# Two-layer hybrid encoder: norm factor of the differential heads by DMA, another order of output tiles, sink as a score column

## The chip, the cores and the metric

The kernel runs on one NeuronCore of a Trainium2 chip. It has a matrix engine (TensorE, PE in the profile, with PEld for its weight loads), a vector engine (DVE), an activation engine (ACT), a general-purpose engine (POOL) and a queue engine (SP) that issues all the DMAs here. Each engine works through its own list of instructions in order and waits on semaphores. The metric is the device time in microseconds of the whole program, median over runs. Three runs of the kernel before took 1253.59 to 1255.1 us, with a median of 1253.75.

## The reference

A two-layer encoder on x of 1024 tokens by 1024 channels in float32, with 256 memory tokens. Each layer: RMS norm, one input projection, several groups of attention heads, a SiLU gate on their outputs, an output projection, and the residual; at the end one more RMS norm.

Layer 0 has three groups of heads of width 64. (A) six windowed heads over 128 tokens to either side, with a relative-position bias and a learned sink logit per head that takes part in the softmax only as an extra column:

```
sink_col = broadcast(sink)                       # one column
p = softmax(concat([logits, sink_col], -1))[..., :-1]
```

(B) six dense heads with RMS-normed queries and keys and rotary positions. (X) four cross-attention heads into the memory.

Layer 1 has (C) six differential heads with values of width 128, and (X) again:

```
p = softmax(s + bias)            # two score maps, i = 0, 1
w = p[0] - lam * p[1]
y_c = rmsnorm(w @ v, subln_g) * (1 - lam_init)
```

so each row of a differential head's output is divided by its own root mean square over 128 channels. That factor is one number per token and head.

## The kernel before, in words

Everything large is computed with split operands: each float32 operand is a high part and a low part, and three matmuls (high-high, high-low, low-high) stand for one (`load_w`, `split_to`). The input projections run as jobs (class `Jobs`) in 24 matmuls per 128 output channels and 512 tokens, into one of two PSUM banks of the ring `A` (`ps_a`, L222). Scores go into one of two double banks of the ring `S` (`ps_s`), and transposes and small results into one of two banks of the ring `T` (`ps_t`).

`run_steps` (L441) goes through the attention as a list of steps; a step is a query block of 128 tokens (B, C, X) or two (A). In iteration i it issues, in this order: the copy `er<-e` of step i-1's probabilities by DMA (`hop`), the scores of step i (`s1`), a share of the projection jobs, the pending follow-ups of earlier steps (`posts`, one piece of each per iteration), the product with the values of a step some iterations back (`s3`), the transposes of step i-2 (`s2`, tile `te`, split by ACT into `PTh` and by DVE into `PTl`), the end of step i's softmax (`finish`), and more jobs. From this program order a scheduler makes each engine's list; it can move an instruction past others.

**Layer 0, B step** (L1044-1070): DVE takes the minimum `mn` of the scores, multiplies it by the query's norm factor into `mr` (L1063), and ACT takes the exponential with `mr` as bias (L1064). **A step** (L1116-1151): DVE adds bias and takes the minimum together with the sink (L1132), ACT takes the exponential and its sum `z` (L1136), then the exponential of the sink, `es` (L1139); DVE adds `es` to `z` (L1141) and takes the reciprocal.

**Layer 1, C step** (L1412-1452) with `s3` at every second step (L1457): 24 matmuls give `oc`, 128 channels by 256 tokens. Follow-up `d1`, one iteration later, sums the squares over the channels with four matmuls (`ssqc`, L1479), two ACT instructions add the epsilon term (L1483) and POOL raises to -1/2 (`rz`, L229). This leaves the factors as a column per block, one token per partition. Follow-up `d2`, another iteration later, has TensorE transpose each column, broadcast to 128x128, so that every partition holds the row of all 128 factors (`rbcc`, L1492); DVE multiplies `O` by it out of PSUM (L1494), and POOL multiplies by the gate (L1497). After the last block of a head the gated output is stored to DRAM (`store_y`).

**Output projection** (`out_proj`, L1216): eight tiles of 128 tokens, in the order `ORD[l]`. Stored outputs come back by DMA (`yr`) and are split; each tile has 48 matmuls of 512 columns. For the tiles in `PRE[l]` a part was already done as filling work during the attention (`pre`, L687): in layer 0 tiles 2 to 5 have 24 matmuls left and tiles 6 and 7 have 12; in layer 1 tiles 2, 3 and 4 have 12 left. `pieces` (L1230) chooses the PSUM banks: a double bank of `S` for all but the last tile, and single banks of `A` and `T` for the last. After a tile's matmuls DVE adds the residual (`x`, L1274), ACT squares and sums (L1275), POOL raises to -1/2, and DVE scales (`xs`, L1295). In layer 0 the scaled tile is then transposed (`tx`, L344) into layer 1's input.

## Time and profile before

| | |
|---|---|
| median of 3 runs | 1253.75 us (1253.59 to 1255.1) |
| profiled execution, its own time | 1255.58 us |
| its span, first to last instruction | 1253.8 us |
| granted TensorE clock | 0.996 |
| busy: PE / DVE / ACT / POOL | 96% / 65% / 51% / 33% |
| layer 0 attention | about 100 to 540 us |
| layer 0 output projection | about 540 to 600 us |
| layer 1 projections, cross-attention | about 600 to 720 us |
| layer 1 differential attention | about 720 to 1184 us |
| layer 1 output projection | about 1184 to 1254 us |

A row of a timeline gives the start in us, the duration, the engine, the source line, the operation, `out<-in`, and in brackets the idle time before it with what ended it. A row of groups gives count, busy time, mean ns of one, and idle time before. In the rows on DMAs come the count, the size of each and the median us from issue to landing.

### The profile page before, as it was taken

How to read it: one execution, taken by the hardware profiler on the slowest of the kernel's cores; microseconds unless marked ns; L12 is line 12 of the kernel's file. 1: busy time of each engine (PE TensorE's matmuls, PEld its weight loads, DVE VectorE, ACT ScalarE, POOL GpSimd, SP SyncE). 2: the span in 40 equal slices, each digit the busy share in tenths (PEclk: the TensorE clock that was granted, in tenths of full speed). 3: DMA queues.
4: the chain of work that ended last, by engine and by line, in shares of the span. 5: the costliest groups of instructions: out<-in, count | busy, mean ns of one | idle time of the engine just before them, and what ended most of it. 6: DMA issues, size and time to landing. Idle time of an engine off the chain costs nothing. (4 is left out here: it accounts for less than half of the span.)

```text
span 1253.8 us, 19637 instructions
## 1 busy us (share of the span) xinstructions
PE 1205.5 (96%) x6806; PEld 999.2 (80%) x6806; DVE 817.1 (65%) x1545; ACT 640.2 (51%) x1395; POOL 413.5 (33%) x390
## 2 busy tenths in 40 slices
PE   5999999999998999998999999999999999999997
PEld 4887788888887787887888778788887878877876
DVE  5547666377778788746355865766667666678444
ACT  6249654256666766533157644444444454456322
POOL 5023456266666565403122212212122131223100
PEclk9999999999999999999999999999999999999999
DMA  6654444545365575466644334243342433445363
GB/s 252 198 187 149 155 168 150 171 155 201 148 224 191 210 246 186 154 203 213 185 163 144 125 107 120 93 143 108 105 137 76 136 115 118 144 151 189 129 211 118
DMA packets 96350, 199.90 MB, mean 159 GB/s; under 512 B 11478, under 2 KB 31190, under 8 KB 96252
## 3 DMA queue, kind: packets, MB, share of 16 engines
q1 hardware_dynamic: 96252, 198.65, 47.4%
q8 instruction: 54, 0.88, 0.3%
q14 instruction: 44, 0.36, 0.1%
HBM read 79.32 MB, written 31.47 MB: 88 GB/s over the span
## 5 line engine op out<-in xcount | busy, mean ns | idle before, releaser
L297 PE MATMUL acc<-h,wh 128*128 128x512 f32 x1536 | 499.1, 399 | 7.3 <-DVE yt L624 3.1
L297 PEld LDWEIGHTS acc<-h,wh 128*128 128x128 f32 x1536 | 283.2, 188 | 73.3 <-issue 13.4
L297 PE MATMUL acc<-h,wl 128*128 128x512 f32 x768 | 304.6, 397 | 1.8 <-POOL wl L241 1.8
L241 POOL TENSOR_TENSOR wl<-wr,wh 128x512 fp32r<-128x512 f32 x96 | 124.9, 1302 | 340.0 <-DVE wh L239 125.2
L316 DVE TENSOR_TENSOR PTl<-te,PTh 128x512 fp32r<-128x512 f32 x224 | 148.2, 687 | 131.2 <-ACT PTh L315 128.4
L1440 ACT ACTIVATE e<-e,mn 128x1024 f32<-128x1024 f32 x96 | 110.2, 1149 | 130.7 <-DVE mn L1437 127.5
L297 PEld LDWEIGHTS acc<-h,wl 128*128 128x128 f32 x768 | 144.8, 189 | 35.5 <-issue 4.4
L315 ACT CAST PTh<-te 128x512 fp32r<-128x512 f32 x224 | 124.9, 591 | 30.2 <-PE te L540 24.6
L1068 POOL TENSOR_TENSOR e<-e,rz 128x1024 f32<-128x1024 f32 x48 | 91.7, 1913 | 78.1 <-DVE rz L1067 66.7
L1437 DVE CUSTOM_DVE_ANT_0 e<-sc,toep 128x1024 f32<-128x1024 f32 x96 | 113.9, 1217 | 5.3 <-PE sc L1431 5.0
L540 PEld LDWEIGHTS te<-identr,er 128*128 128x128 f32 x896 | 91.8, 143 | 21.1 <-issue 4.1
L540 PE MATMUL te<-identr,er 128*128 128x128 f32 x896 | 100.0, 246 | 7.5 <-issue 3.2
L239 DVE CAST wh<-wr 128x512 fp32r<-128x512 f32 x112 | 59.1, 530 | 43.9 <-PE acc L297 14.4
L1064 ACT ACTIVATE e<-sb,mr,nrq 128x1024 f32<-128x1024 f32 x48 | 58.0, 1208 | 48.4 <-DVE mr L1063 33.9
L1449 DVE SCALAR_TENSOR_TENSOR e<-e,mr 128x1024 f32<-128x1024 f32 x48 | 76.2, 1588 | 1.3
L1464 PE MATMUL oc<-PTh,v 128*128 128x256 f32 x384 | 74.8, 288 | 0.3 <-DVE ckl L1333 0.3
L660 PE MATMUL po<-woh,yh 128*128 128x512 f32 (+1 forms) x172 | 65.9, 383 | 1.5 <-DVE x L1274 1.5
L660 PE MATMUL po<-woh,yl 128*128 128x512 f32 (+1 forms) x172 | 65.6, 381 | 0.0
L660 PE MATMUL po<-wol,yh 128*128 128x512 f32 (+1 forms) x172 | 65.5, 381 | 0.0
L1464 PEld LDWEIGHTS oc<-PTh,v 128*128 128x128 f32 x384 | 61.5, 192 | 0.7 <-DVE ckl L1333 0.6
L1059 DVE TENSOR_REDUCE mn<-sb 128x1 f32<-128x1024 f32 x48 | 58.4, 1216 | 5.1 <-PE sb L509 4.7
L318 ACT ACTIVATE yh<-yr 128x256 fp32r<-128x256 f32 (+2 forms) x56 | 24.0, 448 | 67.3 <-DMA yr<-ysc 38.5
(199 smaller groups left out, 2247.1 us busy)
## 6 DMA issues: line engine op xcount, KB each, us to landing
er<-e SPq DMA_DIRECT2D x112, 512.0 KB, 2.9
wr<-in_w_in SPq DMA_DIRECT2D x96, 256.0 KB, 2.8
ysc<-gy SPq DMA_DIRECT2D x16, 512.0 KB, 2.9
wor<-in_w_out SPq DMA_DIRECT2D x32, 256.0 KB, 3.5
cq<-sg SPq DMA_DIRECT2D x64, 128.0 KB, 2.6
ck<-sg SPq DMA_DIRECT2D x48, 128.0 KB, 2.3
er<-e SPq DMA_DIRECT2D x12, 384.0 KB, 2.8
xpsc<-xh SPq DMA_DIRECT2D x18, 256.0 KB, 2.5
```

The lines of the kernel that those rows point to most:

```text
L239: nc.vector.tensor_copy(hi, raw)
L241: (nc.vector if fast else nc.gpsimd).tensor_tensor(out=lo, in0=raw, in1=hi, op=ALU.subtract)
L297: lastmm[0] = nc.tensor.matmul(acc, a, b[:, k, c0:c0 + n], start=(i == 0), stop=(i == 23))
L315: nc.scalar.copy(hi, src)
L316: return nc.vector.tensor_tensor(out=lo, in0=src, in1=hi, op=ALU.subtract)
L540: nc.tensor.transpose(to[:, i * P:(i + 1) * P], e[0][:, k * P:(k + 1) * P], idt)
L660: lastmm[0] = nc.tensor.matmul(acc, a, b, start=(start and n == 0), stop=(stop and n == 2))
L1068: nc.gpsimd.tensor_tensor(out=et, in0=et, in1=rz.to_broadcast([P, 1024]), op=ALU.mult)
L1437: nc.vector.tensor_tensor_reduce(out=et, in0=Sp, in1=toeps[h][:, w0:w0 + 1024], scale=1.0, scalar=BIG, op0=ALU.add, op1=ALU.min, accum_out ...
L1440: nc.scalar.activation(et, et, AF.Exp, bias=mn[:, m:m + 1], scale=-1.0, accum_out=z[:, m:m + 1])
L1449: nc.vector.scalar_tensor_tensor(out=es[0], in0=es[1], scalar=c, in1=es[0], op0=ALU.mult, op1=ALU.add)
L1464: nc.tensor.matmul(acc, V[:, kt, v, :], pt[:, kt, :], start=(n == 0), stop=(n == 23))
```

## The change

Five edits. (1) The row of norm factors reaches all partitions through DRAM: `d1` ends by storing the two columns to `rc_d`, transposed, and `d2` loads them back into `sqc` (whose squares are no longer needed), broadcast to all partitions; the multiply becomes a third follow-up `d3`, one iteration later. The last pair of the last head keeps the transposes. (2) The third tile of an output projection uses the two single banks of `A`. (3) Both orders of output tiles are others. (4) In a B step ACT computes `mr`. (5) In an A step the sink is written by ACT as one more score column behind each block's scores, the exponential and its sum run over that column too, and the separate exponential and addition go; the tile has 770 columns instead of 768.

```
-ORD = ((0, 1, 2, 3, 4, 5, 6, 7), (0, 1, 4, 2, 5, 3, 6, 7))
+ORD = ((0, 1, 2, 6, 3, 7, 4, 5), (0, 1, 5, 2, 6, 3, 4, 7))
...
-                nc.vector.tensor_tensor(out=mr, in0=mn, in1=rq[:, qb, h:h + 1], op=ALU.mult)
+                nc.scalar.activation(mr, mn, AF.Identity, scale=rq[:, qb, h:h + 1])
...
-                et = new_e(M)[:, :768].rearrange("p (j c) -> p j c", j=2)
+                et = new_e(M)[:, :770].rearrange("p (j c) -> p j c", j=2)
...
+                ends = [(min(8, qb + 2) - qb + 1) * P for qb in (2 * p, 2 * p + 1)]
+                if ends[0] == ends[1]:
+                    nc.scalar.copy(et[:, :, ends[0]], nsink[:, h:h + 1].to_broadcast([P, 2]))
+                else:
+                    for j in range(2):
+                        nc.scalar.copy(et[:, j, ends[j]:ends[j] + 1], nsink[:, h:h + 1])
...
-                    nc.scalar.activation(et[:, j, c:c + n], et[:, j, c:c + n], AF.Exp,
+                    nc.scalar.activation(et[:, j, c:c + n + 1], et[:, j, c:c + n + 1], AF.Exp,
                                          bias=mn[:, j:j + 1], scale=-1.0, accum_out=z[:, j:j + 1])
-                es = stat("es", 2)
-                nc.scalar.activation(es, mn, AF.Exp, bias=sinkb[:, h:h + 1], scale=1.0)
                 def finish():
-                    nc.vector.tensor_tensor(out=z, in0=z, in1=es, op=ALU.add)
...
-                t = M.at.tile([P, 1024], F32R, tag="er", name="er", bufs=M.cfg["er"])[:, :768]
-                a, b = (P if p == 0 else 0), (768 - P if p == 3 else 768)
+                t = M.at.tile([P, 1024], F32R, tag="er", name="er", bufs=M.cfg["er"])[:, :770]
+                a, b = (P if p == 0 else 0), (769 - P if p == 3 else 769)
...
         def pieces(i):
+            if i == 2:
+                p = [(ps_a("po")[:, 0:512], c, 512) for c in (0, 512)]
+                return p, p
...
+                    short = h == 5 and qb == 7
...
                         rstd_from(r, v, 2)
                         st_["r"] = r
+                        if not short:
+                            st_["d"] = dr.tile([2, P], F32, name="rc_d")
+                            dma(st_["d"].rearrange("t p -> p t"), r)
 
                     def d2():
-                        T = ps_t("rbcc")
-                        for i in range(2):
-                            nc.tensor.transpose(T[:, i * P:(i + 1) * P],
-                                                st_["r"][:, i:i + 1].to_broadcast([P, P]), ident)
-                        nc.vector.scalar_tensor_tensor(out=O, in0=O, scalar=gs, in1=T[:, 0:256],
+                        dma(sq, st_["d"].rearrange("t p -> (t p)").partition_broadcast(P))
+
+                    def d3():
+                        if short:
+                            T = ps_t("rbcc")[:, :256]
+                            for i in range(2):
+                                nc.tensor.transpose(T[:, i * P:(i + 1) * P],
+                                                    st_["r"][:, i:i + 1].to_broadcast([P, P]), ident)
+                        else:
+                            T = sq
+                        nc.vector.scalar_tensor_tensor(out=O, in0=O, scalar=gs, in1=T,
                                                        op0=ALU.mult, op1=ALU.mult)
...
-                    return [d1, d2]
+                    return [d1, d3] if short else [d1, d2, d3]
```

How the lists of instructions change is shown at three places. First, TensorE in layer 1's attention, at a pair of query blocks of the second head; `acc` is the projection job that fills the time, `oc` the product with the values. Before:

```order
L297 MATMUL acc<-h,wh 128x512 x2
L297 MATMUL acc<-h,wl 128x512
L1492 MATMUL rbcc<-ident,rz_9444 128x128 x2
L1464 MATMUL oc<-PTh,v 128x256
L1464 MATMUL oc<-PTl,v 128x256
L1464 MATMUL oc<-PTh,v 128x256 x2
```

With the change:

```order
L297 MATMUL acc<-h,wh 128x512 x2
L297 MATMUL acc<-h,wl 128x512
L1470 MATMUL oc<-PTh,v 128x256
L1470 MATMUL oc<-PTl,v 128x256
L1470 MATMUL oc<-PTh,v 128x256 x2
```

The two transposes are gone and nothing else has moved here.

Second, SP's queue in the same stage, over some four query blocks (`er` the copy of the probabilities, `wr` a weight load, `ysc` the store of a finished head, `ck` rows of the next head's keys). Before:

```order
L175 DMA wr<-in_w_in 128x512 x2
L175 DMA er<-e 128x1024 x2
L175 DMA wr<-in_w_in 128x512 x2
L175 DMA er<-e 128x1024
L175 DMA ysc_95<-gy 128x1024
```

With the change:

```order
L175 DMA wr<-in_w_in 128x512 x2
L175 DMA rc_d<-rz_9629 128x2x1
L175 DMA sqc<-rc_d 128x256
L175 DMA er<-e 128x1024 x2
L175 DMA wr<-in_w_in 128x512
L175 DMA rc_d<-rz_9818 128x2x1
L175 DMA sqc<-rc_d 128x256
L175 DMA wr<-in_w_in 128x512
L175 DMA er<-e 128x1024
L175 DMA ysc_95<-gy 128x1024
```

Store and load of a pair stand back to back here, ahead of copies and a weight load; at other pairs a weight load, copies or key rows stand between the two.

Third, ACT in layer 0's attention, around A steps and the B steps between them (`yt` and `PT` are the work of earlier steps). Before:

```order
L1136 ACTIVATE e,z_3389<-e,mn_3388 128x384 x2
L1139 ACTIVATE es<-mn_3388,small 128x2
L437 COPY yt<-oa 64x256
L315 CAST PTh<-te 128x4x128 x2
L425 ACTIVATE gy<-acc 128x512
L315 CAST PTh<-te 128x4x128
L1064 ACTIVATE e,z<-sb,mr,nrq 128x1024
L315 CAST PTh<-te 128x4x128
```

With the change:

```order
L1142 ACTIVATE e,z_3380<-e,mn_3379 128x385 x2
L437 COPY yt<-oa 64x256
L315 CAST PTh<-te 128x4x128 x2
L425 ACTIVATE gy<-acc 128x512
L1063 ACTIVATE mr<-mn,rq 128x1
L315 CAST PTh<-te 128x4x128
L1064 ACTIVATE e,z<-sb,mr,nrq 128x1024
```

The exponential of the sink is gone, the exponentials are a column longer, and the scaling `mr` stands ahead of a cast and the B step's exponential. The copies of the sink (`e<-nsink`) stand ahead of the exponentials of their step, here some rows earlier.

## Prediction

> **What bounds the kernel now.** The page's engine shares come first, then the table by stretch, then who waited for whom.
>
> ```profile
> PE 1205.5 (96%) x6806; PEld 999.2 (80%) x6806; DVE 817.1 (65%) x1545; ACT 640.2 (51%) x1395; POOL 413.5 (33%) x390
> ```
>
> ```profile
> 200.00:540.00 340.00, 329.17 (x1974) 280.27 (x1974) 242.59 (x528) 200.96 (x442) 191.49 (x171) 0.99 0.55 190
> 545.00:600.00 55.00, 50.97 (x254) 41.42 (x253) 36.60 (x58) 21.11 (x43) 13.19 (x16) 1.00 0.66 206
> 800.00:1100.00 300.00, 300.00 (x1689) 242.82 (x1688) 206.32 (x361) 141.71 (x280) 65.68 (x66) 1.00 0.36 117
> 1100.00:1184.00 84.00, 81.37 (x477) 65.68 (x475) 62.72 (x111) 47.24 (x101) 20.31 (x19) 1.00 0.47 160
> ```
>
> In the table by stretch the columns are the stretch, its length, the busy time (and count) of PE, PEld, DVE, ACT and POOL, the clock, the DMA share and GB/s. PE is the bound everywhere, and in layer 1's attention, 800 to 1100 us, it never rests: 300.00 of 300. What leaves PE's list there shortens the program one for one, and what is only taken off DVE, ACT or POOL there gives nothing. Elsewhere PE has little idle time: 340.00 - 329.17 = 10.8 us in layer 0's attention and 55.00 - 50.97 = 4.0 us in layer 0's output projection. The waits of PE say whose it is:
>
> ```profile
> PE te L540 <- issue: 3.2, 5, 1.4
> PE sa L509 <- ACT e L1064: 2.1, 2, 1.1
> PE sa L509 <- DVE mn L1132: 1.7, 3, 1.1
> PE tx L344 <- DVE h L316: 1.7, 1, 1.7
> PE po L660 <- DVE x L1274: 1.5, 1, 1.5
> PE pre L660 <- DVE yt L438: 1.2, 1, 1.2
> PE tx L344 <- DVE xs L1295: 1.2, 2, 0.7
> PE acc L297 <- DVE v L1283: 1.1, 1, 1.1
> PE te L540 <- DVE O L1494: 0.8, 1, 0.8
> ```
>
> (Total us, times, longest.) These nine rows are nearly all of what the five edits can win by shortening waits: 14.5 us at the very most.
>
> **1. The norm factor by DMA.** Per pair of query blocks and head, two TensorE transposes (L1492) go, in 23 of 24 pairs; 46 instructions. Their price is read where they stand between two saturated groups, against the one place where the same two groups meet without them:
>
> ```profile
> 795.89 0.39 PE L297 MATMUL acc<-h,wh 128*128 128x512 f32 x1
> 796.12 0.38 PE L1492 MATMUL rbcc<-ident,rz 128*128 128x128 f32 x2
> 796.25 0.36 PE L1464 MATMUL oc<-PTh,v 128*128 128x256 f32 x1
> 796.45 0.28 PE L1464 MATMUL oc<-PTl,v 128*128 128x256 f32 x1
> ...
> 733.39 0.61 PE L297 MATMUL acc<-h,wh 128*128 128x512 f32 x2
> 733.84 0.28 PE L1464 MATMUL oc<-PTh,v 128*128 128x256 f32 x1
> 733.96 0.28 PE L1464 MATMUL oc<-PTl,v 128*128 128x256 f32 x1
> ...
> L1492 PE MATMUL rbcc<-ident,rz 128*128 128x128 f32 x48 | 9.2, 273 | 0.5 <-POOL rz L229 0.5
> ```
>
> Without them the second `oc` starts 0.12 us after the slot that follows `acc` (733.84 to 733.96); with them 0.33 us after it (796.12 to 796.45). So a pair of transposes costs 0.21 us, and 23 pairs cost **4.8 us**. The ends: 0.13 us a pair (796.12 to 796.25, if only the issue slot counts) is 3.0 us; the whole duration of each, 46 x 0.273, is 12.6 us. I take 4.8, since it is a difference of like with like, and the starts show that most of a duration is hidden behind the neighbours.
>
> The Trainium skill, "TensorE: Matmul & The Clock Gate", section Part 4: PE-mode transpose, gives about 275 ns for a 128x128 transpose inside a kernel, and the row's mean of 273 ns agrees. Charged so, an estimate by that page, the transposes would be worth 46 x 0.275 = 12.7 us; that case is among the rivals below.
>
> `rbcc` also leaves the ring of two T banks that `te` uses, so the wait of `te` for DVE's read of it (last row of the waits, 0.8 us, from 0 to 0.8) should go: **0.8 us**.
>
> What is added are two DMAs a pair on SP's queue: `rc_d<-rz` (256 elements of 4 bytes to DRAM, after POOL's `rz`), and `sqc<-rc_d` (128 rows of 1 KB back, after the first has landed); the multiply of `O` and the gate (POOL) move a step later. Behind the waiting SP stand the copies `er<-e`, `wr` and `ck`/`cq`. No DMA of 4-byte elements is in the trace; the nearest rows are
>
> ```profile
> xkl<-xkl SPq DMA_DIRECT2D x8, 64.0 KB, 2.0
> er<-e SPq DMA_DIRECT2D x112, 512.0 KB, 2.9
> PTl<-memT SPq DMA_DIRECT2D x2, 512.0 KB, 8.0
> ...
> 745.73 0.70 POOL L229 TENSOR_TENSOR rz<-z,nhalf 128x2 f32<-128x2 f32 x1 [11.78 <-ACT z L1483]
> 750.18 0.48 SPq L175 DMA_DIRECT2D er<-e  x1
> 765.19 0.52 PE L540 MATMUL te<-identr,er 128*128 128x128 f32 x4
> ...
> 790.66 0.71 POOL L229 TENSOR_TENSOR rz<-z,nhalf 128x2 f32<-128x2 f32 x1
> 794.94 9.18 SPq L175 DMA_DIRECT2D er<-e  x2
> ```
>
> so each lands in 2.0 to 8.0 us, the pair in 4 to 16; I take about 3 each, the row of the commonest copies, since both are small. `rz` is ready at 746.43, and SP then has 3.75 us until its next copy at 750.18; in the pair where store and load stand back to back, `rz` is ready at 791.37 and the next copy starts at 794.94, 3.57 us later. There a store of 3 us is waited out before the load is issued, and the `er` copy leaves at most about 0.5 us late. What is late next can afford it: the copy issued at 750.18 is read by `te` at 765.19 (one step lies between: the group of `te` in between reads the copy before it), so after 2.9 us of flight 12.1 us are left. The moved multiply stands a full step behind the issue of its load. So the DMAs cost **0**; without this cover each pair would cost what the two landings exceed it by, below.
>
> **2. Third tile in the accumulators, new order, layer 1.** In the row `po <- DVE x` the tile that follows a short one (12 matmuls remain where a tile was begun early) finds its two-bank buffer unread: 1.5 us. In the new order the third tile has all 48 matmuls and takes the idle accumulator banks, and no tile reuses a buffer whose reader is less than one tile behind: **1.5 us**, between 0 (a new wait of the same kind for the loads of tile 5, whose second half can only be split once tile 0 releases its buffers) and 1.5.
>
> **3. The same in layer 0.** The order now mixes the short tiles 6 and 7 (12 matmuls) with 24-matmul ones and ends with long ones. The wait of the next projection for the accumulator (`acc <- DVE v`, 1.1 us) should go, because 12 instead of 6 matmuls now separate its bank's evacuation from it. The waits of the transposes for `xs` and `h` (1.7 + 1.2 us) I expect to move rather than end: short tiles now cover long ones' chain of sum, square, power and scale with less. **1.1 us**, between a loss of 2 (every short tile uncovers one `xs`-like wait of 0.7, three of them) and a gain of 4.0, all the idle time of the stretch.
>
> **4. Sink as a score column; `mr` on ACT.**
>
> ```profile
> L1063 DVE TENSOR_TENSOR mr<-mn,rq 128x1 f32<-128x1 f32 x48 | 9.3, 193 | 0.7
> L1141 DVE TENSOR_TENSOR z<-z,es 128x2 f32<-128x2 f32 x24 | 6.9, 286 | 14.0 <-ACT es L1139 13.9
> L1139 ACT ACTIVATE es<-mn,small 128x2 f32<-128x2 f32 x24 | 6.8, 281 | 0.0
> L1483 ACT ACTIVATE z<-ssqc,es 128x1 f32<-128x1 f32 x48 | 10.0, 258 | 4.5 <-PE ssqc L1479 4.3
> ```
>
> DVE loses 9.3 + 6.9 us of work and 13.9 us of standing still for `es`. ACT loses 6.8 and gains 48 scalings and 30 tiny copies at about 0.26 us each by the L1483 row: 78 x 0.258 = 20.1, so 13.3 more on an engine that was busy for 201 of 340 us. Off the path both; the path sees only PE's waits on these engines, in the stretch from 200 to 540: 3.2 + 2.1 + 1.7 + 1.2 = 8.2 us of the list above. Against a gain: in 13 of 48 B steps a `PTh` cast now stands behind a scaling that waits for DVE's minimum. I take a little under a fifth, **1.5 us**, between a loss of 4 (half of 8.2 again, by that ACT queue) and a gain of 4. The copies of 769 instead of 768 columns are hidden as the others are.
>
> **Sum:** 4.8 + 0.8 + 1.5 + 1.1 + 1.5 = 9.7 us. The profiled execution took 1255.58 us for a span of 1253.8 (1.8 lies around it) and would take 1245.9; it stands 1.8 above the median of the runs, 1253.75, which becomes **1244.0**.
>
> **Rivals.**
> - *Only the transposes pay.* The waits are reshuffled, not ended: 1253.75 - 4.8 = 1249.0. For it: the waits are single events of about 1 us, in an order of instructions that shifts everywhere in layer 0. Against: two of them have a named buffer that the edit frees. 20%.
> - *The new order costs in layer 0.* Term 4 at -4 and term 3 at -2, the rest as forecast: 7.1 - 6 = 1.1 us gained, 1252.6, no change. For it: ACT's queue, above. Against: DVE, the busier one, loses 30 us of work and waiting. 8%.
> - *The transposes cost their whole duration*: 12.6 + 0.8 + 1.5 + 1.1 + 1.5 = 17.5, so 1236.2. For it: PE's list is saturated, and 9.2 us of busy time stands on the group. Against: the starts differ by 0.21 us a pair, not 0.55. 6%.
> - *Slower: SP's round trip decides.* Place: SP's queue in layer 1. The cover is 3.6 us up to the next copy plus 12.1 us until PE reads it, 15.7 in all; store and load together longer than that stop PE once a pair. The 9.7 us are eaten from 9.7 / 23 = 0.42 us a pair, so from 16.1 us. With both at the bound of 8.0 us it is 16.0, no loss yet; at 17 the price is 23 x 1.3 = 30, so 1244.0 + 30 = 1274. For it: element-wise stores are new, and SP is in order. Against: 8.0 us is the longest median of any row of issues, and of 512 KB. 6%. The Trainium skill, "DMA: Bandwidth & Descriptors", section Specifications, speaks against the change: below 512 bytes a transfer is a read-modify-write; it states no time for that, and no run shown so far has such a store.
>
> The forecast itself has 60%.
>
> **How the numbers follow.** The forecast's own range is 1241 to 1247. With the first rival at 1249 and part of the second and third, the range is 1239.5 to 1251.5; outside lie the slow round trip, the whole-duration case and half of the second. About 0.2%, 2.5 us, is what a measurement tells from no change: faster means below 1251.2. Faster: 60 + 20 + 6 = 86; same: 8; slower: 6.
>
> **What would show it.** Term 1: in 800 to 1100 PE stays at 300 of 300 and the distance from one pair's `oc` to the next falls by 0.21 us, with no wait of PE on `er`; `rc_d` lands in about 3 us. Term 2: no `po` wait on DVE `x`. Term 3: no `acc` wait on `v`, but `tx` waits remain. Term 4: PE idle in layer 0's attention near 9 us, not 15. The forecast is wrong if PE waits for `te` behind late `er` copies, or if layer 0's attention grows by more than 3 us.

## The result and the profile after

The changed kernel takes 1313.05 us (1306.93 to 1315.06, 6 runs) against 1252.99 us (1250.91 to 1255.1, 6 runs) for the kernel before: ratio 1.0472, 95% interval 1.0448 to 1.0497. It is 60 us slower where 9.7 us less were forecast. The profiled execution has a span of 1311.5 us. Among the runs of the experiments below, one of the four of e13 took 2308.86 us and is left out of its ratio; the other three took 1268.48 to 1273.07 us.

The table by stretch of the changed kernel, with the columns of the prediction (stretch, length, busy time and count of PE, PEld, DVE, ACT and POOL, clock, DMA share, GB/s):

```profile
200.00:540.00 340.00, 329.94 (x1972) 282.85 (x1972) 234.46 (x463) 208.08 (x488) 190.03 (x169) 0.99 0.55 192
545.00:600.00 55.00, 51.22 (x253) 41.22 (x252) 36.84 (x58) 21.76 (x45) 13.29 (x16) 1.00 0.69 220
800.00:1100.00 300.00, 281.54 (x1528) 223.82 (x1526) 191.86 (x334) 129.21 (x258) 61.03 (x62) 0.97 0.41 112
1100.00:1240.00 140.00, 110.11 (x572) 86.92 (x568) 77.80 (x134) 55.79 (x119) 20.88 (x22) 0.89 0.39 127
```

In layer 0 the shares are as they were, and layer 1's first copy of `O` (see below) even comes 5.3 us earlier, at 731.64 against 736.92. In layer 1's attention, where PE never rested (300.00 of 300, 1689 matmuls), it is now busy for 281.54 of 300 us, with 1528 matmuls. The waits of DVE, PE and SP in the changed kernel (total us, times, longest):

```profile
DVE O L1510 <- DMA sqc<-rc_d: 124.2, 22, 8.3
DVE PTl L316 <- ACT PTh L315: 61.6, 70, 4.5
...
PE te L540 <- ACT z L1490: 18.2, 10, 3.6
...
PE pre L660 <- ACT sqc L1475: 8.0, 1, 8.0
PE ssqc L1486 <- ACT sqc L1475: 5.2, 1, 5.2
PE tv L405 <- DVE PTl L316: 4.8, 4, 1.7
...
SPq L175 <- DMA rc_d<-rz: 137.0, 23, 9.3
```

The rows of its two new DMAs (count, size, median us from issue to landing):

```profile
sqc<-rc_d SPq DMA_DIRECT2D x23, 128.0 KB, 4.5
rc_d<-rz SPq DMA_DIRECT2D x23, 1.0 KB, 7.3
```

Two waits are new and large: DVE's multiply of `O` waits 124 us for the load of the factor, and SP waits 137 us for the store. The store of 1 KB lands in 7.3 us and the load in 4.5. How this comes about shows in the timelines of POOL, SP and DVE around one pair (start, duration, engine, in brackets the idle time before and what ended it):

```profile
825.59 0.70 POOL L229 TENSOR_TENSOR rz<-z,nhalf 128x2 f32<-128x2 f32 x1
...
826.32 0.38 SPq L175 DMA_DIRECT2D rc_d<-rz  x1
832.85 0.32 SPq L175 DMA_DIRECT2D sqc<-rc_d  x1
...
833.31 0.08 DVE L1443 DVE_READ_ACCUMULATOR2_ANT mn<- 128x1 f32 x1
837.25 0.49 DVE L1510 SCALAR_TENSOR_TENSOR O<-O,misc,sqc 128x256 f32<-128x256 f32 x1 [3.86 <-DMA sqc<-rc_d]
837.65 1.28 DVE L316 TENSOR_TENSOR PTl<-te,PTh 128x512 fp32r<-128x512 f32 x2
```

`rz` is ready at 826.29. DVE comes to the multiply at 833.39, 7.1 us later, since in its list the multiply stands directly behind the next scores and ahead of the split `PTl`, as in the kernel before, and not a step later, as in the program's text. The factor is there at 837.25, 11.0 us after `rz`. `PTl`, the softmax's end and the next scores all stand behind it.

In this pair PE's other matmuls cover the wait of 3.86 us: the interval from one copy of `O` to the next, 836.12 to 857.28, takes 21.2 us, and 21.4 in the kernel without the DMAs. The wait reaches PE where it is longer, as two pairs earlier (timelines of DVE, ACT and PE):

```profile
797.10 0.48 DVE L1510 SCALAR_TENSOR_TENSOR O<-O,misc,sqc 128x256 f32<-128x256 f32 x1 [6.57 <-DMA sqc<-rc_d]
...
802.20 1.15 ACT L1446 ACTIVATE e<-e,mn 128x1024 f32<-128x1024 f32 x1 [5.40 <-DVE mn L1443]
...
804.50 0.39 ACT L1490 ACTIVATE z<-ssqc,es 128x1 f32<-128x1 f32 x2
...
804.94 0.54 PE L540 MATMUL te<-identr,er 128*128 128x128 f32 x4 [2.09 <-ACT z L1490]
```

The next scores come late on DVE, so ACT's exponential comes late, and `z` stands behind it on ACT. `z` reads `ssqc`, which shares the two banks of the ring `T` with `te`, and PE stands 2.09 us for the bank. That is the row `te <- ACT z` of the waits. In the 15 intervals of the next paragraph PE stands in ten, 18.5 us in all, each with a wait of DVE of 4.7 us or more; the five with a wait of 4.6 us or less cost nothing.

For the accounting I use the copies of `O` on ACT, one per pair (24 of them). The timeline of ACT gives the third, the eighteenth and the last, first in the changed kernel and then in the kernel without the DMAs (the first experiment, e1):

```profile
774.80 0.37 ACT L1473 COPY O<-oc 128x256 f32<-128x256 f32 x1 [2.35 <-PE oc L1470]
1096.38 0.37 ACT L1473 COPY O<-oc 128x256 f32<-128x256 f32 x1 [1.38 <-PE oc L1470]
1237.02 0.35 ACT L1473 COPY O<-oc 128x256 f32<-128x256 f32 x1
```

```profile
776.44 0.37 ACT L1473 COPY O<-oc 128x256 f32<-128x256 f32 x1 [2.57 <-PE oc L1470]
1073.44 0.37 ACT L1473 COPY O<-oc 128x256 f32<-128x256 f32 x1 [1.62 <-PE oc L1470]
1177.56 0.37 ACT L1473 COPY O<-oc 128x256 f32<-128x256 f32 x1 [0.84 <-PE oc L1470]
```

The 15 intervals from the third to the eighteenth, in which PE is full of filling matmuls, I call the full stretch: 321.6 us against 297.0. The last six intervals, where the projection jobs run out, are the thin stretch: 140.6 against 104.1. The difference of the spans, 1311.5 - 1248.0 = 63.5, is 24.6 in the full stretch, 36.5 in the thin one, 4.0 behind the last copy and 1.6 the other way ahead of the third.

### The profile page after: what moved, and what is told of

Its sections match the earlier page's. It is cut to its first block, busy times and chain, and to the rows that moved or that the text cites. A ratio compares the mean times of both kernels' runs of the same rounds, so it can differ in the third digit from the quotient of the medians.

```text
span 1311.5 us, 19659 instructions
## 1 busy us (share of the span) xinstructions
PE 1221.6 (93%) x6760; PEld 1008.4 (77%) x6760; DVE 809.4 (62%) x1479; ACT 649.0 (49%) x1453; POOL 412.3 (31%) x390
## 5 line engine op out<-in xcount | busy, mean ns | idle before, releaser
L1446 ACT ACTIVATE e<-e,mn 128x1024 f32<-128x1024 f32 x96 | 110.1, 1148 | 163.9 <-DVE mn L1443 163.3
L316 DVE TENSOR_TENSOR PTl<-te,PTh 128x512 fp32r<-128x512 f32 x224 | 148.2, 685 | 63.2 <-ACT PTh L315 61.6
L540 PE MATMUL te<-identr,er 128*128 128x128 f32 x896 | 100.4, 248 | 25.5 <-ACT z L1490 18.2
L1443 DVE CUSTOM_DVE_ANT_0 e<-sc,toep 128x1024 f32<-128x1024 f32 x96 | 113.9, 1216 | 5.9 <-PE sc L1437 5.7
L1513 POOL TENSOR_TENSOR gy<-O,gy 128x256 f32<-128x256 f32 x24 | 17.6, 735 | 245.9 <-DVE O L1510 210.4
L1510 DVE SCALAR_TENSOR_TENSOR O<-O,misc,sqc 128x256 f32<-128x256 f32 x23 | 11.2, 485 | 124.2 <-DMA sqc<-rc_d 124.2
## 6 DMA issues: line engine op xcount, KB each, us to landing
cq<-sg SPq DMA_DIRECT2D x64, 128.0 KB, 3.3
ck<-sg SPq DMA_DIRECT2D x48, 128.0 KB, 2.8
```

Of the source, the lines that this page charges most:

```text
L316: return nc.vector.tensor_tensor(out=lo, in0=src, in1=hi, op=ALU.subtract)
L540: nc.tensor.transpose(to[:, i * P:(i + 1) * P], e[0][:, k * P:(k + 1) * P], idt)
L1443: nc.vector.tensor_tensor_reduce(out=et, in0=Sp, in1=toeps[h][:, w0:w0 + 1024], scale=1.0, scalar=BIG, op0=ALU.add, op1=ALU.min, accum_out ...
L1446: nc.scalar.activation(et, et, AF.Exp, bias=mn[:, m:m + 1], scale=-1.0, accum_out=z[:, m:m + 1])
```

## The experiments

Each is built on the changed kernel or on the kernel before. The table gives the two stretches of every kernel from its trace, the times follow below it.

| kernel | full, us | thin, us |
|---|---|---|
| before | 296.7 | 104.2 |
| changed | 321.6 | 140.6 |
| e1, no DMAs | 297.0 | 104.1 |
| e2, DMAs alone | 322.3 | 141.5 |
| e3, multiply behind the scores | 298.4 | 130.7 |
| e4, DMAs unread | 302.0 | 128.0 |
| e5, e3 with the last six by TensorE | 298.3 | 105.2 |
| e6, e3 with 8-byte rows | 293.6 | 109.8 |
| e7, e3 on GpSimd's queue | 293.6 | 120.4 |
| e8, new orders alone | 296.7 | 104.3 |
| e9, e6 with the last six by TensorE | 293.6 | 104.8 |
| e10, 8-byte rows alone | 293.6 | 112.1 |
| e11, sink column and `mr` alone | 297.0 | 104.0 |
| e12, four forms of store, unread | 297.0 | 113.0 |
| e13b, stores alone | 297.0 | 121.3 |
| e14, loads alone | 297.0 | 105.8 |
| e15, 8-byte stores alone | 296.9 | 110.1 |

**Which edit: e1, the DMAs taken back; e2, the DMAs alone.**

e1 against the changed kernel:

```diff
-                            dma(st_["d"].rearrange("t p -> p t"), r)
-                        dma(sq, st_["d"].rearrange("t p -> (t p)").partition_broadcast(P))
+                        T = ps_t("rbcc")
+                        for i in range(2):
+                            nc.tensor.transpose(T[:, i * P:(i + 1) * P],
+                                                st_["r"][:, i:i + 1].to_broadcast([P, P]), ident)
...
-                    return [d1, d3] if short else [d1, d2, d3]
+                    return [d1, d2]
```

e2 against the kernel before, the first edit of the change and nothing else (in both cuts the lines around these are left out):

```diff
+                            dma(st_["d"].rearrange("t p -> p t"), r)
+                        dma(sq, st_["d"].rearrange("t p -> (t p)").partition_broadcast(P))
+                    return [d1, d3] if short else [d1, d2, d3]
```

> The changed kernel with its first edit taken back: the norm factor reaches the partitions by TensorE's two transposes again, the other four edits stay. Theory D (VectorE's list: the multiply of O stands ahead of the split PTl and waits for the load of the factor) and theory S (SP's queue: the load's wait for the store holds up the copies behind it) both say that the loss goes with this edit: layer 0 was 5.3 us faster in the changed kernel, so about 1253 - 5.3 = 1247.5, from 1245 to 1250, with a distance of some 381 us from the copy of O at 794 us to the last one, as before. Theory O (the new orders, the sink column or mr on ScalarE cost the time): 1300 or more.

> The kernel before with the first edit alone: two DMAs in place of the two transposes, the multiply moved. Theories D and S: the whole loss of layer 1's attention, 61 us, without the 5.3 us that layer 0 gained: about 1253 + 61 = 1314, from 1306 to 1320; VectorE waits for the factor's load some 120 us in all. Theory O: within 8 us of the kernel before, below 1260.

e1 takes 1249.76 us, ratio to the kernel before 0.9963 (0.9948 to 0.9979). e2 takes 1319.01 us, 1.0516 (1.0499 to 1.0533), and its DVE waits 121.1 us for the load. The whole loss belongs to the DMAs, and the other four edits gain 4.6 us, as theories D and S have it; theory O is out.

**Place in the list or SP's queue: e3, the multiply one step later on DVE; e4, the DMAs without a reader.**

e3 against the changed kernel (`lastsc[0]` is the DVE score instruction, L1443, that was written last):

```diff
-                        nc.vector.scalar_tensor_tensor(out=O, in0=O, scalar=gs, in1=T,
-                                                       op0=ALU.mult, op1=ALU.mult)
+                        with tc.issue_after(lastsc[0].ins):
+                            nc.vector.scalar_tensor_tensor(out=O, in0=O, scalar=gs, in1=T,
+                                                           op0=ALU.mult, op1=ALU.mult)
```

e4 against the changed kernel, with the transposes in all pairs, so that the load's data stay unread:

```diff
-                        if short:
-                            T = ps_t("rbcc")[:, :256]
+                        T = ps_t("rbcc")[:, :256]
...
-                        else:
-                            T = sq
...
-                    return [d1, d3] if short else [d1, d2, d3]
+                    return [d1, d3] if short else [d1, lambda: (d2(), d3())]
```

> The changed kernel, with the multiply of O held behind VectorE's score instructions of the step in which the program writes it (one step later in VectorE's list: about 10 us); DMAs and SP's queue as they are. Theory D: the multiply then finds the factor landed (4.5 us after the load's issue, against about 10), VectorE's wait for it falls from 124 to under 15 us, and the time is that of the changed kernel without the 61 us and with the 4.8 us of the transposes: 1243 to 1248. Theory S: SP still stands 137 us for the stores, the copies er and wr stay late, and the time stays at 1295 or more.

> The changed kernel with store and load on SP as they are, but the multiply takes the factor from TensorE's two transposes, as in the kernel before; what the load brings is read by nobody. So SP still waits for each store, and VectorE waits for no load. Theory D: as without the DMAs, 1246 to 1250. Theory S: 1300 or more, with waits of PE for er. In between, each theory has the share that the time shows.

e3 takes 1281.88 us, 1.0223 (1.0193 to 1.0252); e4 takes 1276.43 us, 1.0175 (1.0156 to 1.0195). Neither theory had its number, and DVE's wait accounts for most of one stretch only. In e3 DVE's wait is nearly gone, and most of the loss of the full stretch with it (298.4 us), while SP waits on and the thin stretch keeps 26.6 us of its loss:

```profile
DVE PTl L316 <- ACT PTh L315: 134.4, 83, 5.6
...
DVE O L1512 <- DMA sqc<-rc_d: 11.8, 2, 9.9
```

```profile
SPq L175 <- DMA rc_d<-rz: 113.7, 21, 8.5
```

DVE's own waiting for `PTh` is back at 134 us, beside 61.6 in the changed kernel: of the 124 us that DVE waited for the load some 73 fell into time in which it would have waited anyway. In e4 no engine needs the load, and 27 us are lost all the same, 24 of them in the thin stretch. Something other than DVE costs there.

**Where SP's part lies: e5, TensorE's transposes again in the last six pairs only.**

Against e3:

```diff
-                    short = h == 5 and qb == 7
+                    short = 4 * h + qb // 2 >= 18
```

> As the kernel with the multiply behind the scores, but the last six pairs of layer 1 (from the second half of the fifth head on, where fewer matmuls are left to fill in) take the factor from TensorE's transposes; 18 pairs keep their DMAs. By the copies of O, that kernel lost 26.5 us in its last six pairs against the kernel without DMAs, and 1.4 us in the 15 intervals ahead of them, with single intervals 0.2 us shorter. Theory S, bounded to the thin stretch (SP's wait for a store costs only where PE has no other matmuls queued): 1246 to 1251, level with the kernel without DMAs at 1249.8 or up to 3 us below it. If SP's wait costs everywhere: 1265 or more.

It takes 1251.41 us, 0.9982 (0.9966 to 0.9999), 0.4 us above the range expected. The thin stretch is nearly whole again (105.2), though SP still waits 88.7 us for the 18 stores that are left. In the full stretch these pairs have no transposes, and yet it is 1.3 us longer than in e1. Beside the kernels below that lack the transposes too and wait less (293.6 us), SP's wait costs 4.7 us there in e5 and 4.8 in e3; e4, which keeps the transposes, has 5.0 us over e1.

**What makes the landing long: e6, 8-byte rows behind the scores; e10, 8-byte rows with the multiply where it was.**

The same lines, in e6 against e3 and in e10 against the changed kernel:

```diff
-                            st_["d"] = dr.tile([2, P], F32, name="rc_d")
-                            dma(st_["d"].rearrange("t p -> p t"), r)
+                            st_["d"] = dr.tile([P, 2], F32, name="rc_d")
+                            dma(st_["d"], r)
-                        dma(sq, st_["d"].rearrange("t p -> (t p)").partition_broadcast(P))
+                        dma(sq, st_["d"].rearrange("p t -> (p t)").partition_broadcast(P))
-                            T = sq
+                            T = sq.rearrange("q (p t) -> q t p", t=2)
```

> As the kernel with the multiply behind the scores, in all 23 pairs, but the store is 128 rows of 8 bytes and not 256 elements of 4 (the factor's two values of a partition beside each other; the load brings them interleaved and the multiply reads with a stride). If the number of small pieces sets the landing: the store lands in about half, 3 to 5 us against 7, SP waits some 60 us instead of 114, and the time falls by about 10 us, to 1268 to 1275. If the landing is a fixed time for any small store: 7 us as before and 1278 to 1286.

> The changed kernel with 8-byte rows alone: the multiply stays ahead of PTl in VectorE's list. Theory L (the landing is the cause, the place in the list only hands it on): store and load now land in 3.4 + 4.0 = 7.4 us instead of 11.8, so VectorE's wait of 5.6 us a pair shrinks by 4.4 to about 1.2, some 15 to 35 us in all, and the time is 1250 to 1262. Theory P (the place ahead of PTl costs the time whatever the landing): VectorE still waits 3 us or more a pair, 1280 or more.

e6 takes 1252.81 us, 0.9987 (0.9973 to 1.0002), 29 us below e3, three times the gain expected. e10 takes 1254.97 us, 1.0004 (0.9989 to 1.0019): theory L. The store's row in e6, then store and load in e10:

```profile
rc_d<-rz SPq DMA_DIRECT2D x23, 1.0 KB, 3.4
```

```profile
rc_d<-rz SPq DMA_DIRECT2D x23, 1.0 KB, 3.3
sqc<-rc_d SPq DMA_DIRECT2D x23, 128.0 KB, 4.3
```

And from e10's waits of DVE:

```profile
DVE O L1510 <- DMA sqc<-rc_d: 43.4, 21, 4.5
```

With 7.6 us for both, DVE's wait at the same place in its list falls to 2.1 us a pair and costs nothing in the full stretch, which takes 293.6 us whether the multiply is ahead of `PTl` or a step later. With 11.8 us the place was worth 31 us (1313 to 1282); with 7.6 us it is worth 2, which is within the two intervals.

**Another queue: e7, both DMAs issued by GpSimd.**

Against e3:

```diff
-                            dma(st_["d"].rearrange("t p -> p t"), r)
+                            dma(st_["d"].rearrange("t p -> p t"), r, nc.gpsimd)
-                        dma(sq, st_["d"].rearrange("t p -> (t p)").partition_broadcast(P))
+                        dma(sq, st_["d"].rearrange("t p -> (t p)").partition_broadcast(P), nc.gpsimd)
```

> As the kernel with the multiply behind the scores, but both DMAs are issued by GpSimd, which computes the factor, and not by SP. Theory S: SP no longer waits for any store and the copies er, wr and wor leave as without the DMAs, so the 27 to 32 us come back: 1246 to 1255, unless the wait only moves: GpSimd's weight splits wl and wol now stand behind the load, and where PE waits for wl or wol the time stays above 1265. If SP's wait was not the cause of what remains: 1275 to 1285.

It takes 1272.49 us, 1.014 (1.0119 to 1.016). SP no longer waits for a store, the full stretch is whole (293.6), and the thin one still loses 16.3 us. The time lies between what was expected with SP's wait as the cause and without it, and above 1265 not for the reason named there: PE waits only 0.9 us for `wl`. GpSimd stands 118.9 us for the stores in SP's place, and the copies `er`, issued by SP, land late too. The landing of `er` in the 295 us from 780 on (min, median, max), here from the other queue:

```profile
DMA to landing us min/median/max: 2.8/5.3/9.9
```

The same answer for e1 gives 2.8, 2.9 and 3.6. So while slow stores, and loads, are under way on one queue, copies from another land late; which of the two delays them is for e13b and e14 below. The Trainium skill, "DMA: Bandwidth & Descriptors", section Issuing engines are not separate DMA queues, says that DMAs run on the same 16 engines whatever engine issues them, and these late copies of the other queue agree with that.

**Piece or number: e12, four forms of store that nobody reads, in e1.**

Against e1, in `d1`:

```diff
+                        k = (4 * h + qb // 2) % 4
+                        if k == 0:
+                            dma(dr.tile([2, P], F32, name="fa").rearrange("t p -> p t"), r)
+                        elif k == 1:
+                            dma(dr.tile([P, 2], F32, name="fb"), r)
+                        elif k == 2:
+                            dma(dr.tile([P, 1], F32, name="fc"), r[:, 0:1])
+                        else:
+                            dma(dr.tile([2, P, 2], F32, name="fd").rearrange("t p m -> p t m"),
+                                grp["z"].rearrange("p (t m) -> p t m", m=2))
```

> The changed kernel with TensorE's transposes and, in each pair, one store that nobody reads, in four forms by turns: 256 pieces of 4 bytes, 128 rows of 8 bytes, 128 pieces of 4 bytes, 256 pieces of 8 bytes; no load and no wait. If the number of pieces sets the landing: 7, 3.5, 3.5 and 7 us. If the size of a piece does: 7, 3.5, 7 and 3.5 us. The time within 4 us of the kernel without DMAs, since nothing waits.

The rows of the four stores:

```profile
fa<-rz SPq DMA_DIRECT2D x6, 1.0 KB, 7.9
fb<-rz SPq DMA_DIRECT2D x6, 1.0 KB, 2.9
fd<-mn SPq DMA_DIRECT2D x6, 2.0 KB, 4.2
fc<-rz SPq DMA_DIRECT2D x6, 0.5 KB, 6.7
```

256 pieces of 4 bytes land in 7.9 us, 128 of 4 bytes in 6.7, 256 of 8 bytes in 4.2, 128 of 8 bytes in 2.9. The piece's size decides (3.7 to 3.8 us between 4 and 8 bytes). The number seems to add 1.2 to 1.3 us, but that is not shown: each form always stands at the same pair of a head, and the landing of one and the same store (e13b) has medians from 7.2 to 8.5 us at these four places. The second reading was nearer. The time, 1258.37 us in one run, is 8.6 above e1, outside what was expected: stores that nobody reads cost time too, which the next runs follow up.

**The slow store by itself: e13, the stores alone; e13b, the same for its trace; e14, the loads alone; e15, stores of 8-byte rows alone.** All are unread.

e13 and e13b against e1, in `d1`; e15 has the store of e6 in the same place:

```diff
+                        if not (h == 5 and qb == 7):
+                            dma(dr.tile([2, P], F32, name="rc_d").rearrange("t p -> p t"), r)
```

e14 against e1, in `d2` (`rc0` is written once at the start):

```diff
+                        if not (h == 5 and qb == 7):
+                            dma(sq, rc0.rearrange("t p -> (t p)").partition_broadcast(P))
```

> The kernel without DMAs (the other four edits, TensorE's transposes), with the 23 stores of 256 pieces of 4 bytes added on SP; nobody reads them and there is no load, so SP waits for no landing. Theory W (SP's wait for the landing is the cost): as without them, 1248 to 1252, though er and wor may land later. Theory E (transfers behind a slow store land late, and that stops PE in the thin stretch): 1260 to 1277; er lands in about 5 us and not 2.9, wor and yr in up to 10.

> The kernel without DMAs, with the 23 loads of 128 KB alone, from a tensor written once at the start; nobody reads them and SP waits for no store. All theories: 1248 to 1252, since 128 KB is a quarter of an er copy and lands in about 4 us. Above 1255 the load would have a share of its own.

> The same kernel as the run of the stores alone (23 stores of 256 pieces of 4 bytes, no load, no reader), for its trace. Theory E (transfers behind a slow store land late): 1266 to 1276; er lands in about 5 us against 2.9; of the 22 us lost against the kernel without DMAs, 15 or more lie in the last six pairs, and ScalarE waits there for wor and yr. If instead the 15 intervals ahead of them lose as much, the thin stretch is not what decides.

> The kernel without DMAs, with the 23 stores alone, but each of 128 rows of 8 bytes. Theory E with the piece's size as the cause: 1249 to 1253, level with the kernel without DMAs, er at about 3 us. If any small store does this: 1260 to 1272.

e13: ratio 1.0125 (1.0098 to 1.0153); e13b: 1269.1 us in one run. So 23 stores of 1 KB, which nobody waits for, cost about 20 us: theory E. Of the 19.3 us between the spans of e13b and e1, 17.1 lie in the thin stretch and none in the full one, though copies land late there too. The median of `er` over the 295 us is 3.3 us, not the 5 expected, but it mixes two kinds. By the issues and landings in e13b's trace from 720 to 1180 us, the 17 `er` copies that were in flight together with a store landed in 6.7 us at the median, the other 21 in 2.9. How it reaches PE, from e13b's timelines of SP, ACT, DVE and PE:

```profile
1127.91 0.38 SPq L175 DMA_DIRECT2D rc_d<-rz  x1
1129.45 4.58 SPq L175 DMA_DIRECT2D wor<-in_w_out  x3
...
1140.02 0.62 ACT L257 CAST woh<-wor 128x512 fp32r<-128x512 f32 x1 [9.62 <-DMA wor<-in_w_out]
...
1141.56 0.97 DVE L258 TENSOR_TENSOR wol<-wor,woh 128x512 fp32r<-128x512 f32 x1 [6.60 <-ACT woh L257]
1142.45 0.47 DVE L1502 SCALAR_TENSOR_TENSOR O<-O,misc,rbcc 128x256 f32<-128x256 f32 x1
...
1142.97 0.75 PE L540 MATMUL te<-identr,er 128*128 128x128 f32 x4 [7.70 <-DVE O L1502]
```

The weights `wor`, issued 1.5 us behind the store, land late (up to 11.0 us against 4.4 at most in e1). ACT's list stands at their cast `woh` for 9.62 us. DVE's split `wol` waits for the cast, the multiply of `O` stands behind it on DVE, and `te` needs the bank that the multiply reads. PE has no projection matmuls left to fill the 7.70 us, and `pre`, the filling work that is left, needs the late weights itself. This is one stop; the others were not followed one by one.

e14: 1251.93 us, 0.9978 (0.9962 to 0.9995), thin stretch +1.7: the load by itself is nearly free, and `er` lands in 2.9 us. Where SP has waited for a store first (e6), the 15 `er` copies in flight with a load and no store landed in 5.1 us at the median, so a load is not harmless everywhere; the full stretch doesn't show it. e15: 1258.41 us, 1.0036 (1.0022 to 1.0049), thin stretch +5.9; this misses the 1249 to 1253 expected. 8-byte stores do a third of the harm in the thin stretch, and not quite half by the ratios, not none. The store has the same place on SP in e13b and e15, and SP waits as long for `rz` ahead of it (14.8 and 14.1 us in all), so the difference between the two is the piece's size and not the place in the queue.

**The other four edits: e8, the new orders with the third tile in the accumulators; e11, the sink column with `mr` on ACT.**

e8 against the kernel before:

```diff
-ORD = ((0, 1, 2, 3, 4, 5, 6, 7), (0, 1, 4, 2, 5, 3, 6, 7))
+ORD = ((0, 1, 2, 6, 3, 7, 4, 5), (0, 1, 5, 2, 6, 3, 4, 7))
...
+            if i == 2:
+                p = [(ps_a("po")[:, 0:512], c, 512) for c in (0, 512)]
+                return p, p
```

e11 against the kernel before, with the sink's column as in the change and the old orders:

```diff
-                nc.vector.tensor_tensor(out=mr, in0=mn, in1=rq[:, qb, h:h + 1], op=ALU.mult)
+                nc.scalar.activation(mr, mn, AF.Identity, scale=rq[:, qb, h:h + 1])
...
-                et = new_e(M)[:, :768].rearrange("p (j c) -> p j c", j=2)
+                et = new_e(M)[:, :770].rearrange("p (j c) -> p j c", j=2)
```

> The kernel before with the new order of output tiles in both layers and the third tile in the accumulators, and nothing else. The four edits beside the DMAs gained 4.7 us together. The prediction's terms for these: 1.5 + 1.1 = 2.6 us, so 1252 to 1252.5 against a kernel before at 1254.5. The rival that the order costs 2 us in layer 0: 1255 to 1257.

> The kernel before with the sink as a score column and mr on ScalarE, and nothing else. All four edits beside the DMAs gained 4.7 us (interval 2.6 to 6.5), the new orders alone 2.1 (0.4 to 3.8). If the gains add: 2.6 us, a ratio of about 0.998; the prediction's term is 1.5 us; the rival that ScalarE's queue costs: 1255 to 1258.

e8: 1251.94 us, 0.9983 (0.997 to 0.9997), a gain of 2.1 us (0.4 to 3.8). e11: 1252.25 us, 0.9987 (0.9975 to 0.9998), a gain of 1.6 us (0.3 to 3.1). The two add to 3.7 of the 4.6 us that e1 shows.

**What the findings make together: e9, 8-byte rows, multiply behind the scores, TensorE's transposes in the last six pairs.**

Against e6:

```diff
-                    short = h == 5 and qb == 7
+                    short = 4 * h + qb // 2 >= 18
```

> The three findings together: the store in 128 rows of 8 bytes, the multiply behind the scores, and the last six pairs with TensorE's transposes. By the copies of O, the kernel with 8-byte rows ran its saturated intervals 0.2 us shorter than the kernel without DMAs (293.5 us for 15 against 297.0) and lost 5.6 us in the last six. So this one should stand 18 x 0.2 = 3.6 us below the kernel without DMAs, at 1245 to 1248, if a kernel before of 1253 to 1254.5 runs beside it (ratio 0.993 to 0.997). If the transposes are free after all: level with the kernel without DMAs, ratio 0.996 to 0.998.

e9 takes 1246.58 us, 0.9938 (0.9923 to 0.9954), as expected: faster than the kernel before by 7.7 us, than the changed one by 66 us, and some 3 us below e1. From its table by stretch:

```profile
800.00:1100.00 300.00, 300.00 (x1674) 242.25 (x1673) 213.40 (x367) 142.21 (x281) 69.57 (x66) 1.00 0.42 126
```

From its timeline of ACT, the same three copies of `O`:

```profile
778.13 0.37 ACT L1474 COPY O<-oc 128x256 f32<-128x256 f32 x1 [2.34 <-PE oc L1471]
1071.70 0.37 ACT L1474 COPY O<-oc 128x256 f32<-128x256 f32 x1 [1.40 <-PE oc L1471]
1176.54 0.38 ACT L1474 COPY O<-oc 128x256 f32<-128x256 f32 x1 [2.16 <-PE oc L1471]
```

PE is full again, and the full stretch takes 293.6 us, 3.4 less than without the DMAs.

## Why the prediction was wrong

**Term 1, the transposes: right.** "0.21 us" per pair was forecast; where PE waits for nothing that the DMAs hold up (e6, e9, e10) the 15 intervals are 3.4 us shorter than in e1, 0.23 us each. The rival that charged their whole duration (0.55 us a pair) is out. The wait of `te` for DVE's `O` is in e1 (0.8 us) and not in e6.

**Term 1, the DMAs at 0: the step that failed.** Two statements in it were wrong. First, "I take about 3 each": the store took 7.3 us and the load 4.5, so 11.8 in place of 6. The bounds from 2.0 to 8.0 held both; the choice within them went by the commonest copies, which are rows of kilobytes, for a store of 4-byte pieces. That a DMA is quick because it is small had a row of the trace against it, though an unclean one, since loads of 512 KB stood ahead of it:

```profile
tab<-in_rel_bias SPq DMA_DIRECT2D x1, 0.8 KB, 5.2
```

Second, "The moved multiply stands a full step behind the issue of its load". That was read from the program's text. In DVE's list the multiply stands where it stood before, ahead of `PTl`. In the full stretch DVE reached it 4.3 to 8.4 us after `rz` was ready (7.1 in the pair shown), and the factor was there after 11.0 to 13.6. The 15.7 us of cover were counted along SP and `er` to PE; the shorter way, through DVE, was not counted. Along it PE's other matmuls cover some 4.6 us more, so the 6 us of the forecast would have cost the full stretch nothing; in e10 7.2 to 9.9 us from `rz` to the multiply cost it nothing.

The loss of the full stretch, 28.0 us against the 293.6 without it, needed both the slow landing and the early place. Mending the landing alone (e10) brings all of it back, mending the place alone (e3) 23.2 us; the 4.8 that stay go with SP's wait, since they are gone in e7, whose stores are as slow but where SP doesn't wait. The sign that the prediction named for its failure, `te` behind late `er` copies, is not among PE's waits in the changed kernel; PE's waits for `te` there end with ACT's `z` (18.2 us).

**The slower rival: near in place, wrong in mechanism.** It priced SP's round trip from 16.1 us on, where PE waits for `er` once a pair. The trip took 11.8 us at the medians and stayed below that point, and in the full stretch SP's wait of 5 to 6 us a pair costs some 5 us in all (e3, e4, e5). What costs is the thin stretch, and there neither SP's wait nor `er` is the largest part, but the slow store itself, which holds up other transfers: 17.1 us with stores alone, 6.7 more with the loads and SP's wait for the stores (e4), 9.9 more in the changed kernel than in e3, where DVE's wait is taken away. These shares come from different kernels and need not add exactly. The prediction cut layer 1's attention at 1100 us in its own table (81.37 of 84 there) and then let one pair stand for all 23.

**Terms 2 and 3: right together, within the error.** 1.5 + 1.1 = 2.6 us forecast, 2.1 measured (0.4 to 3.8); no run parts the two. The wait of `po` for DVE's `x` is not among the changed kernel's waits, nor that of `acc` for `v`; the waits of `tx` remained, as said, at 3.1 to 3.7 us.

**Term 4: right in size, but not where the trace was to show it.** 1.5 us forecast, 1.6 measured (0.3 to 3.1). The sign "PE idle in layer 0's attention near 9 us" can't be read at this size: from 200 to 540 us PE is idle for 8.9 us in e11, 10.1 in the changed kernel and 11.0 in e1, which have the edit, and for 10.8 before, 10.1 in e2 and 9.7 in e8, which don't. From the first B scores to the first tile of the output projection it is 385.8 to 387.5 us in the three with the edit and 387.8 to 390.1 in the three without, one execution each; this agrees with a gain there and doesn't prove it. The rival that the new order or ACT's queue costs in layer 0 is out.

**The sum.** With the DMAs at their forecast price the sum holds within the error: e9, which makes that price nearly true in 18 pairs, gains 7.7 us (5.8 to 9.7), where the terms give 9.7 - 5 x 0.21 = 8.7.

## What to carry to other kernels

Price a new DMA by its smallest contiguous piece, not by its bytes, and look for what else is in flight behind it. Read the place of a moved instruction in its engine's own list, and count the cover from the earliest reader in any list, not along the path that one has in mind. Price each stretch with its own spare work: what is free where PE has filling matmuls can cost all of its length where they have run out.

## What was not expected of the hardware

A store's landing went from 2.9 us to 6.7 when its 128 pieces had 4 bytes and not 8; why, no run here tells. While stores of 4-byte pieces are under way, other transfers land late: `er` at a median of 6.7 us and not 2.9 beside the stores alone (e13b), and `wor` in up to 11.0 where it took 4.4 at most. In e7, with the stores and loads on the other queue, `er` has a median of 5.3.

A stop of PE costs more than its length. From e13b's table by stretch, around the end of the wait of 7.70 us shown above, at 1142.97:

```profile
1140.00:1143.00 3.00, 0.03 (x1) 0.03 (x1) 1.37 (x2) 2.71 (x5) 1.27 (x1) 0.53 1.01 392
1143.00:1147.00 4.00, 4.00 (x12) 3.29 (x13) 2.62 (x7) 3.34 (x8) 0.74 (x1) 0.50 0.83 299
1147.00:1150.00 3.00, 3.00 (x14) 1.91 (x13) 3.00 (x6) 0.00 (x0) 0.00 (x0) 0.99 0.69 207
```

The granted clock falls during the stop, is 0.50 in the 4 us behind it and 0.99 in the next 3. If those 4.00 busy us would shrink in proportion to the clock, the stop cost some 2 us more than it lasted (an estimate from this row). The Trainium skill, "TensorE: Matmul & The Clock Gate", section Why this matters for your kernels, warns of idle gaps above about 3 us for this reason. This row agrees, but shorter stops do it here too: behind the stop of 2.09 us shown in the result, which ended at 804.94, the clock of the changed kernel is 0.62 over 4 us, while behind one of 1.69 us, which ended at 861.44, it stays at 1.00.

```profile
805.00:809.00 4.00, 4.00 (x14) 2.97 (x14) 3.10 (x6) 1.55 (x3) 1.82 (x3) 0.62 0.23 66
```

What this came to in the full stretch shows in the changed kernel, first, beside e6, whose full stretch has the same 1647 matmuls:

```profile
774.80:1096.38 321.58, 303.12 (x1647) 240.98 (x1645) 206.29 (x360) 138.85 (x277) 65.00 (x66) 0.97 0.39 107
773.08:1066.64 293.56, 293.56 (x1647) 237.35 (x1645) 207.94 (x360) 140.66 (x277) 69.76 (x66) 1.00 0.41 121
```

Of the 28.0 us between them PE stands for 18.5, and the other 9.6 are the same matmuls taking longer, at a clock of 0.97 and not 1.00.
